# Low parts of a layer's first weights on VectorE, the last tile of a stage normalised there in halves, and a residual scale folded into a power

## The chip, the cores and the metric

The kernel runs on one core of one Trainium2 chip. The metric is the device time of one execution in microseconds (us). Engines are named as the profile names them: PE (TensorE matmul), PEld (its weight load), DVE (VectorE), ACT (ScalarE), POOL (GpSimd), SP (SyncE, whose queue issues nearly all DMAs).

## The reference

Two layers over 512 latent tokens (x) and 256 context tokens (ctx) of width 1024. A layer has a mixing part (one input projection `w_in`, three head groups, one output projection `w_out`) and a channel part (SwiGLU, `w_up` and `w_down`), each with adaLN modulation in front and DeepNorm post-normalisation behind. Cut to what the change touches:

```python
def layer_norm(x, g=None, b=None):
    mu = mean(x); var = mean((x - mu) ** 2)
    y = (x - mu) * rsqrt(var + 1e-6)
    return y if g is None else y * g + b

for l in range(2):
    hl = layer_norm(xl) * (1 + mod_l[:, 1]) + mod_l[:, 0]
    yl = mixing(hl @ w_in[l]) @ w_out[l]
    xl = layer_norm(ALPHA * xl + mod_l[:, 2] * yl, ln1_g[l], ln1_b[l])
    hl = layer_norm(xl) * (1 + mod_l[:, 4]) + mod_l[:, 3]
    xl = layer_norm(ALPHA * xl + mod_l[:, 5] * swiglu(hl), ln2_g[l], ln2_b[l])
    # the context goes the same way in layer 0; layer 1 only reads its normalised, modulated form
```

The output is the latent stream.

## The kernel before, in words

**Tiles and products.** Tokens lie in six tiles of 128 x 1024: tiles 0 and 1 are context, 2 to 5 latent. Every fp32 product is made of three matmuls over a high and a low part of each operand (`mm`; all PE rows stand at L137). A weight arrives by DMA as a "unit" (512 KB, 128 x 1024), in the order that `plan` lists and that `pump` issues on SP's queue when the heap has room. `split` then makes the high part, on ACT (L211) or on POOL (L213), and the low part as source minus high part (`tt`, L206), on DVE or POOL. For a token tile the high part is made at L671 (ACT) and the low part at L206 too. Which engine makes a unit's parts is set by `self.weng` and `self.wsub`. `mixing` sets POOL for the low parts at its start.

**What sets the order.** `STEPS[l]` is a string that orders the steps of the mixing part of layer l, one letter a step. Z, H, D and the like are both steps and switches: D puts later low parts on DVE, O puts them on POOL, H and h put high parts on POOL or ACT. A small letter such as a, e, f runs a piece of the input projection or the gating; Z starts the products of the first units. A scheduler then sets each engine's own order from the data and from buffer reuse, and an engine runs its list strictly in that order.

**Stage ends.** `ends` closes a sub-layer. Per tile it makes the second product (`project`, two halves of 512 columns), adds the residual (L1251 multiplies by the gate, L206 adds), collects statistics (L715), and calls `post_ln`: `ln_end` aggregates (L635), makes the inverse deviation with a multiply-add on DVE (L236) and a power on POOL (L237), multiplies it by ALPHA for the next residual (L639), and two DVE instructions of 128 x 1024 apply it (L683, L684). `normal` then takes statistics of the result (L629, L635, L236, L237), forms the bias (L649, DVE, 128 x 1) and normalises the whole tile on ACT (L650). `modulate` transposes the tile on PE in eight 128 x 128 blocks (rows `aux<-cst,f`), applies scale and shift on ACT (L665), and makes high and low parts. Modulation of a tile is put two tiles later, and the last two tiles' low parts are on DVE, the others' on POOL.

While the last two tiles are being normalised, PE is fed with `fill`: the first products of the next sub-layer on tiles that are ready (128 x 256 rows), in three pieces set by `cuts`. Three ends have a sub-layer behind them: the end of mixing in layer 0 ("mixing-0 end", 255 to 335 us of the span, six tiles), of the channel part in layer 0 ("MLP-0 end", 846 to 935 us, six tiles), of mixing in layer 1 ("mixing-1 end", 1060 to 1127 us, four tiles). The fourth end writes the output and has neither ALPHA nor `normal`.

The first products of layer 1 in the MLP-0 end use the units z0 and z1 (`in1.z0`, `in1.z1`), a2, a3 and, a little later, v0 and v1. At the entry of the mixing-1 end the eight units of `w_out` are scaled by a column of `par` while they are split (L1384 on ACT, L1385 on DVE).

**Head.** `first_mod` modulates the input of layer 0 in eight column blocks k. Per block, context (128 x 256) and latent (128 x 512) go through a DVE multiply-add (L418), an ACT high part (L422) and a low part: latent on DVE, context on POOL (both L206).

## Time and profile before

| what | value |
|---|---|
| device time, median of 3 runs | 1481.41 us (1479.87 to 1483.12) |
| the profiled execution's own time | 1483.5 us |
| its span (first to last instruction) | 1481.4 us |
| PE busy | 1403.3 us, 95% of the span, 7307 matmuls |
| DVE busy | 865.3 us, 58% |
| ACT busy | 517.4 us, 35% |
| POOL busy | 288.2 us, 19% |
| mean granted TensorE clock | 0.975 of full speed |
| DMA | 160.39 MB, 34.5% of 16 engines' span |

An engine row of a timeline gives the start in the span, the time to the end of the last of the merged instructions, the line, the operation with output and inputs, the count, and in brackets the idle time in front with what ended it. `f` and `r` are heap buffers (fp32, and fp32 in the form that PE takes), `smalls` holds 128 x 1 values, `mm` and `aux` are PSUM. The granted clock is 1.00 at 2.4 GHz and 0.50 at 1.2 GHz.

### The profile page before, as it was taken

The page shows a single profiled execution, that of the slowest core. Times are in us where ns is not written, and L with a number is a line of the kernel's source. Part 1 is how long each engine was busy: PE and PEld are TensorE (multiplying, and loading weights), DVE is VectorE, ACT ScalarE, POOL GpSimd, SP SyncE. Part 2 cuts the span into 40 slices and gives each one's busy share as a digit, 9 for nine tenths or more (in the row PEclk, how much of TensorE's full clock was granted, in tenths as well). Part 3 has the DMA queues.
Part 4 walks back from the last instruction along what each step waited for, and adds up shares of the span by engine and source line. Part 5 has one row for each costly group of instructions (what it writes and reads, how often), then busy time and mean ns, then how long its engine had stood idle before and what let it go on. Part 6 is the DMA issues. An engine that isn't in the chain of part 4 may idle for free.

```text
span 1481.4 us, 18151 instructions
## 1 busy us (share of the span) xinstructions
PE 1403.3 (95%) x7307; PEld 1172.6 (79%) x7307; DVE 865.3 (58%) x1230; ACT 517.4 (35%) x719; POOL 288.2 (19%) x199
## 2 busy tenths in 40 slices
PE   6998898999999999999999998997889999999997
PEld 3777876789888888888888877776678888888885
DVE  6638847779248357536226496579786353362427
ACT  4467435345113203112103155785345232232210
POOL 3302323330030030120030055033330112020201
PEclk9999999999999999999999999998899999999999
DMA  9602455044126053371145015013346143342101
GB/s 325 206 15 89 141 187 183 0 147 154 43 66 204 29 153 117 100 222 63 29 128 185 29 53 147 15 43 100 114 143 198 43 128 114 93 121 78 50 15 57
DMA packets 168419, 160.39 MB, mean 108 GB/s; under 512 B 10344, under 2 KB 126536, under 8 KB 168336
## 3 DMA queue, kind: packets, MB, share of 16 engines
q1 hardware_dynamic: 168224, 158.95, 34.5%
q8 instruction: 57, 0.93, 0.3%
q0 software_dynamic: 112, 0.30, 0.1%
q14 instruction: 26, 0.21, 0.0%
HBM read 157.12 MB, written 2.10 MB: 107 GB/s over the span
## 4 chain that ended last, share of the span: by engine, by line
PE 76%; DVE 12%; ACT 5%; issue 4%; POOL 3%; DMA 1%; SPq 0%; DVEq 0%; ACTq 0%; POOLq 0%
PE mm L137 71%; PE aux L137 5%; POOL smalls L237 2%; DVE f L206 1%; DVE f L684 1%; POOL r L206 1%; DVE r L206 1%; DVE f L1251 1%; DVE f L831 1%; DVE smalls L715 1%; ACT f L665 1%; DVE f L828 1%; DVE r L1385 1%; DVE f L830 1%; ACT f L818 1%
## 5 line engine op out<-in xcount | busy, mean ns | idle before, releaser
L137 PE MATMUL mm<-r,r 128*128 128x512 f32 (+1 forms) x6000 | 1198.0, 361 | 20.2 <-DVE f L1251 6.5
L137 PEld LDWEIGHTS mm<-r,r 128*128 128x128 f32 x6000 | 1009.6, 191 | 198.0 <-DVE f L1251 11.3
L211 ACT ACTIVATE r<-f 128x1024 fp32r<-128x1024 f32 (+2 forms) x210 | 195.0, 953 | 560.2 <-PE mm L137 197.2
L206 DVE TENSOR_TENSOR r<-f,r 128x1024 fp32r<-128x1024 f32 (+2 forms) x232 | 252.1, 1109 | 148.4 <-ACT r L211 123.7
L206 POOL TENSOR_TENSOR f<-f,f 128x1024 f32<-128x1024 f32 x40 | 99.6, 2490 | 636.4 <-DVE f L1251 606.2
L1251 DVE TENSOR_TENSOR f<-mm,f 128x512 f32<-128x512 f32 (+1 forms) x80 | 76.3, 953 | 133.2 <-PE mm L137 132.6
L1266 DVE TENSOR_TENSOR f<-mm,f 128x768 f32<-128x768 f32 (+1 forms) x44 | 36.2, 824 | 169.2 <-PE mm L137 167.5
L206 POOL TENSOR_TENSOR r<-f,r 128x512 fp32r<-128x512 f32 (+2 forms) x52 | 90.0, 1738 | 136.9 <-DVE f L828 45.9
L237 POOL TENSOR_TENSOR smalls<-smalls,neghalf 128x1 f32<-128x1 f32 (+3 forms) x61 | 61.9, 1016 | 246.0 <-DVE smalls L236 245.6
L579 DVE SCALAR_TENSOR_TENSOR f<-f,stc,f 128x512 f32<-128x512 f32 x140 | 102.3, 762 | 5.7 <-DMA f<-in_w_mod_dram 4.5
L206 DVE TENSOR_TENSOR f<-f,f 128x512 f32<-128x512 f32 (+1 forms) x70 | 58.3, 835 | 20.2 <-ACT f L799 18.7
L137 PE MATMUL aux<-r,r 128*128 128x256 f32 x480 | 60.7, 288 | 3.6 <-ACT f L1010 3.6
L137 PEld LDWEIGHTS aux<-r,r 128*128 128x128 f32 x480 | 59.7, 196 | 4.9 <-ACT f L1010 3.8
L665 ACT ACTIVATE f<-aux,modT 128x128 f32<-128x128 f32 x128 | 48.4, 464 | 33.6 <-PE aux L137 31.3
L1265 ACT ACTIVATE f<-mm 128x768 f32<-128x768 f32 (+1 forms) x44 | 30.7, 697 | 77.3 <-PE mm L137 77.2
L137 PE MATMUL aux<-cst,f 128*128 128x128 f32 (+1 forms) x239 | 35.3, 284 | 22.7 <-ACT f L650 12.0
L137 PE MATMUL mm<-f,f 128*128 128x512 f32 (+3 forms) x168 | 52.8, 467 | 4.0 <-ACT f L799 3.0
L650 ACT ACTIVATE f<-f,smalls 128x1024 f32<-128x1024 f32 x19 | 23.6, 1244 | 93.2 <-DVE smalls L649 93.2
L137 PEld LDWEIGHTS aux<-cst,f 128*128 128x128 f32 (+1 forms) x239 | 28.1, 144 | 31.4 <-ACT f L650 14.6
L137 PEld LDWEIGHTS mm<-f,f 128*128 128x128 f32 x168 | 30.9, 193 | 21.0 <-issue 8.6
L783 DVE SCALAR_TENSOR_TENSOR f<-mm,par,f 128x255 f32<-128x255 f32 (+3 forms) x48 | 25.7, 611 | 21.8 <-ACT f L777 21.8
L799 ACT ACTIVATE f<-mm,par 128x768 f32<-128x768 f32 x32 | 28.3, 902 | 15.7 <-PE mm L137 10.7
(128 smaller groups left out, 731.1 us busy)
## 6 DMA issues: line engine op xcount, KB each, us to landing
f<-in_w_mod_dram SPq DMA_DIRECT2D x96, 512.0 KB
f<-in_w_up_dram SPq DMA_DIRECT2D x88, 512.0 KB
f<-in_w_down_dram SPq DMA_DIRECT2D x40, 512.0 KB
f<-in_w_in_dram SPq DMA_DIRECT2D x28, 512.0 KB
f<-in_w_out_dram SPq DMA_DIRECT2D x16, 512.0 KB
f<-in_b_mod_dram SPq DMA_DIRECT2D x6, 512.0 KB
f<-in_x_dram SPq DMA_DIRECT2D x4, 512.0 KB
f<-in_ln_g_dram SPq DMA_DIRECT2D x4, 512.0 KB
```

Source lines behind the costliest of these rows:

```text
L137: i = f(*args, **kw)
L206: return eng.tensor_tensor(out=out, in0=a, in1=b, op=op)
L211: i = self.nc.scalar.activation(h, src, AF.Copy)
L237: self.nc.gpsimd.tensor_tensor(out=out, in0=v, in1=self.neghalf[:, 0:n], op=ALU.pow)
L579: nc.vector.scalar_tensor_tensor(out=b.f, in0=w, scalar=c, in1=b.f, op0=ALU.mult, op1=ALU.add)
L650: nc.scalar.activation(n.f, x, AF.Identity, bias=nm, scale=r)
L665: nc.scalar.activation(y.f[:, q * P : (q + 1) * P], ps[:, q * P : (q + 1) * P], AF.Identity, bias=self.modT[:, slot, k, s : s + 1], scale= ...
L783: nc.vector.scalar_tensor_tensor(out=o, in0=ps[:, i0 : i0 + o1 - o0], scalar=w(k), in1=o, op0=ALU.mult, op1=ALU.add)
L799: insts.append(nc.scalar.activation(g.f, ps[:, 256:1024], AF.Sigmoid, bias=par[:, col : col + 1]))
L1251: self.nc.vector.tensor_tensor(out=tb.f, in0=ps[:, c], in1=m[:, c], op=ALU.mult)
L1265: nc.scalar.activation(g.f, pg[:, 256 + lo : 1024], AF.Silu)
L1266: nc.vector.tensor_tensor(out=g.f, in0=pu[:, 256 + lo : 1024], in1=g.f, op=ALU.mult)
```

## The change

There are four edits:

1. The order string of layer 1 gets a D in front and an O behind the f: the low parts of the units used from there to the O are made on DVE instead of POOL.
2. `first_mod` makes the context's eight low parts on DVE instead of POOL.
3. `ln_end` takes ALPHA into the multiply-add in front of the power, (v q + eps q)^(-1/2) with q = 1 / ALPHA^2, and drops L639, 16 instances.
4. `ends` normalises the last tile of each end that isn't the kernel's last with two DVE instructions of 128 x 512 (`normal_halves`, L655 of the changed file) instead of L649 and L650.

```diff
-STEPS = ("feaeZeeppzssz8shgpmOsgs6p7sVsshvUv6HuvDcLmu8F6gHDc8cFwhuNRmtgDmAQmBmP", "ZaHfeepzszVpssvcecegwsvppUDsFuhugsgDsgs6L7NAtQBP")
+STEPS = ("feaeZeeppzssz8shgpmOsgs6p7sVsshvUv6HuvDcLmu8F6gHDc8cFwhuNRmtgDmAQmBmP", "DZaHfOeepzszVpssvcecegwsvppUDsFuhugsgDsgs6L7NAtQBP")
...
-                self.tt(nc.vector if s == 0 else nc.gpsimd, L, y, H.bitcast(F32), ALU.subtract)
+                self.tt(nc.vector, L, y, H.bitcast(F32), ALU.subtract)
...
-        self.rstd(mv[:, 2:3], mv[:, 1:2], 1.0, eps)
-        r = mv[:, 2:3]
-        if scale is not None and scale != 1.0:
-            nc.vector.tensor_scalar(out=mv[:, 3:4], in0=r, scalar1=scale, scalar2=None, op0=ALU.mult)
-            r = mv[:, 3:4]
-        return mv[:, 0:1], r
+        q = 1.0 / (scale or 1.0) ** 2
+        self.rstd(mv[:, 2:3], mv[:, 1:2], q, eps * q)
+        return mv[:, 0:1], mv[:, 2:3]
...
+    def normal_halves(self, x):
+
+        mu, r = self.ln_stats(x, EPS_X)
+        n = self.buf(D)
+        for c in (slice(0, 512), slice(512, 1024)):
+            self.nc.vector.tensor_scalar(out=n.f[:, c], in0=x[:, c], scalar1=mu, scalar2=r, op0=ALU.subtract, op1=ALU.mult)
+        return n
...
-                ns[ti] = self.normal(self.X[ti])
+                ns[ti] = self.normal_halves(self.X[ti]) if i > len(tiles) - 2 else self.normal(self.X[ti])
```

Behind L639 the changed file's line numbers differ: L649 is L646 there, L650 is L647, L665 and L671 are L670 and L676, L683 and L684 are L688 and L689, L715 is L720, L1251 is L1256, L1384 and L1385 are L1389 and L1390.

**First place: DVE in the MLP-0 end, tile 5.** `f_1024_75` is tile 5; `r_1024` outputs of L206 are low parts of weight units, `r_4096_79` the low part of the tokens. DVE before:

```order
L683 SCALAR_TENSOR_TENSOR f_1024_5869<-f_1024_75,smalls,f_1024_457 128x1024
L639 TENSOR_SCALAR smalls<-smalls 128x1
L206 TENSOR_TENSOR r_1024_5257<-f_1024_5513,r_1024_4714 128x1024
L684 SCALAR_TENSOR_TENSOR f_1024_75<-f_1024_5869,smalls,f_1024_5864 128x1024
L629 BN_STATS smalls<-f_1024_75 128x6 x2
L206 TENSOR_TENSOR r_4096_79<-f_512_6294,r_4096_77 128x512
L635 BN_AGGR smalls<-smalls 128x2
L236 TENSOR_SCALAR smalls<-smalls 128x1
L649 SCALAR_TENSOR_TENSOR smalls<-smalls 128x1
L206 TENSOR_TENSOR r_4096_79<-f_512_5991,r_4096_77 128x512
```

and with the change:

```order
L688 SCALAR_TENSOR_TENSOR f_1024_5863<-f_1024_75,smalls,f_1024_457 128x1024
L206 TENSOR_TENSOR r_1024_5251<-f_1024_5507,r_1024_4708 128x1024
L689 SCALAR_TENSOR_TENSOR f_1024_75<-f_1024_5863,smalls,f_1024_5858 128x1024
L206 TENSOR_TENSOR r_1024_6111<-f_1024_131,r_1024_3692 128x1024
L629 BN_STATS smalls<-f_1024_75 128x6 x2
L206 TENSOR_TENSOR r_4096_79<-f_512_6288,r_4096_77 128x512
L635 BN_AGGR smalls<-smalls 128x2
L206 TENSOR_TENSOR r_1024_4421<-f_1024_4625,r_1024_6969 128x1024
L236 TENSOR_SCALAR smalls<-smalls 128x1
L206 TENSOR_TENSOR r_4096_79<-f_512_5985,r_4096_77 128x512
L655 TENSOR_SCALAR f_1024_5863<-f_1024_75,smalls 128x512 x2
L206 TENSOR_TENSOR r_1024_6242<-f_1024_5791,r_1024_6964 128x1024
```

L639 and L649 are gone, two L655 stand in place of ACT's L650, and two low parts of weight units (`L206 r_1024`, 128 x 1024) that POOL made now stand between the second post-norm instruction and the normalisation. On POOL, in the same place, before:

```order
L237 TENSOR_TENSOR smalls<-smalls,neghalf 128x1
L213 TENSOR_SCALAR r_1024_7057<-f_1024_6817 128x1024
L206 TENSOR_TENSOR r_1024_7058<-f_1024_6817,r_1024_7057 128x1024
L206 TENSOR_TENSOR r_4096_79<-f_512_6294,r_4096_77 128x512
L206 TENSOR_TENSOR r_4096_79<-f_512_6275,r_4096_77 128x512
L237 TENSOR_TENSOR smalls<-smalls,neghalf 128x1 x2
L206 TENSOR_TENSOR r_1024_6117<-f_1024_131,r_1024_3698 128x1024
L237 TENSOR_TENSOR smalls<-smalls,neghalf 128x1
L206 TENSOR_TENSOR r_1024_4427<-f_1024_4631,r_1024_6981 128x1024
L206 TENSOR_TENSOR r_1024_6248<-f_1024_5797,r_1024_6976 128x1024
L213 TENSOR_SCALAR r_1024_5517<-f_1024_459 128x1024
```

and with the change:

```order
L237 TENSOR_TENSOR smalls<-smalls,neghalf 128x1
L213 TENSOR_SCALAR r_1024_7045<-f_1024_6805 128x1024
L237 TENSOR_TENSOR smalls<-smalls,neghalf 128x1
L257 MEMSET f_1024_4415 128x1024
L206 TENSOR_TENSOR r_1024_7046<-f_1024_6805,r_1024_7045 128x1024
L206 TENSOR_TENSOR r_4096_79<-f_512_6288,r_4096_77 128x512
L206 TENSOR_TENSOR r_4096_79<-f_512_6269,r_4096_77 128x512
L237 TENSOR_TENSOR smalls<-smalls,neghalf 128x1 x3
L213 TENSOR_SCALAR r_1024_5511<-f_1024_459 128x1024
```

The three low parts of weight units behind the powers (`r_1024_6117`, `r_1024_4427`, `r_1024_6248`) are gone from POOL, the high part of v1 (L213) has moved in front of a power, and v1's low part and tile 3's two stay ahead of the powers of tiles 4 and 5. PE's list changes there only in its pieces: between tile 4's transposes and tile 5's stand 49 products of 128 x 256 (44 before), and behind tile 5's 131 (141 before).

**Second place: DVE at the entry of the mixing-1 end.** L1385 (L1390) makes the low part of a `w_out` unit, `L206 r_1024` that of a `w_up` unit, `f_1024_192` is the last `w_out` unit to arrive. Before:

```order
L1385 SCALAR_TENSOR_TENSOR r_1024_6256<-f_1024_6179,par,r_1024_7826 128x1024
L206 TENSOR_TENSOR r_1024_7844<-f_1024_7816,r_1024_7843 128x1024
L206 TENSOR_TENSOR r_1024_6248<-f_1024_5797,r_1024_7854 128x1024
L1385 SCALAR_TENSOR_TENSOR r_1024_4418<-f_1024_192,par,r_1024_3121 128x1024
L206 TENSOR_TENSOR r_1024_7177<-f_1024_4356,r_1024_4702 128x1024
L1385 SCALAR_TENSOR_TENSOR r_1024_7841<-f_1024_7814,par,r_1024_7839 128x1024
L1251 TENSOR_TENSOR f_512_7884<-mm,f_1024_3453 128x512
```

and with the change:

```order
L1390 SCALAR_TENSOR_TENSOR r_1024_7335<-f_1024_7542,par,r_1024_7798 128x1024
L1390 SCALAR_TENSOR_TENSOR r_1024_6250<-f_1024_6173,par,r_1024_7814 128x1024
L1390 SCALAR_TENSOR_TENSOR r_1024_7820<-f_1024_7621,par,r_1024_7818 128x1024
L1390 SCALAR_TENSOR_TENSOR r_1024_4412<-f_1024_192,par,r_1024_7828 128x1024
L206 TENSOR_TENSOR r_1024_4422<-f_1024_2650,r_1024_7831 128x1024
L206 TENSOR_TENSOR r_1024_2845<-f_1024_7805,r_1024_3887 128x1024
L206 TENSOR_TENSOR r_1024_3978<-f_1024_4294,r_1024_7841 128x1024
L206 TENSOR_TENSOR r_1024_7046<-f_1024_6805,r_1024_4696 128x1024
L1256 TENSOR_TENSOR f_512_7871<-mm,f_1024_3447 128x512
```

The `w_out` parts now stand together, four low parts of `w_up` behind them, and all of it in front of the first residual. On SP's queue one of the two last `w_out` loads is issued earlier, in front of most `w_up` loads.

**Third place: DVE in the mixing-1 end, tile 5.** Before:

```order
L1251 TENSOR_TENSOR f_512_7055<-mm,f_1024_3453 128x512
L206 TENSOR_TENSOR f_1024_75<-f_1024_75,f_512_7055 128x512
L206 TENSOR_TENSOR r_1024_8393<-f_1024_7829,r_1024_7841 128x1024
L715 BN_STATS smalls<-f_1024_75 128x6
L206 TENSOR_TENSOR r_1024_7057<-f_1024_70,r_1024_8500 128x1024
L635 BN_AGGR smalls<-smalls 128x2
L236 TENSOR_SCALAR smalls<-smalls 128x1
L683 SCALAR_TENSOR_TENSOR f_1024_7989<-f_1024_75,smalls,f_1024_3701 128x1024
L639 TENSOR_SCALAR smalls<-smalls 128x1
L684 SCALAR_TENSOR_TENSOR f_1024_75<-f_1024_7989,smalls,f_1024_7850 128x1024
L629 BN_STATS smalls<-f_1024_75 128x6 x2
L577 TENSOR_SCALAR f_512_5388<-f_1024_192,stc 128x512
```

and with the change:

```order
L1256 TENSOR_TENSOR f_512_8016<-mm,f_1024_3447 128x512
L206 TENSOR_TENSOR f_1024_75<-f_1024_75,f_512_8016 128x512
L720 BN_STATS smalls<-f_1024_75 128x6
L635 BN_AGGR smalls<-smalls 128x2
L236 TENSOR_SCALAR smalls<-smalls 128x1
L688 SCALAR_TENSOR_TENSOR f_1024_7973<-f_1024_75,smalls,f_1024_7836 128x1024
L689 SCALAR_TENSOR_TENSOR f_1024_75<-f_1024_7973,smalls,f_1024_7837 128x1024
L629 BN_STATS smalls<-f_1024_75 128x6 x2
L635 BN_AGGR smalls<-smalls 128x2
L236 TENSOR_SCALAR smalls<-smalls 128x1
L577 TENSOR_SCALAR f_512_8408<-f_1024_4350,stc 128x512
L655 TENSOR_SCALAR f_1024_457<-f_1024_75,smalls 128x512 x2
```

Both low parts of `w_up` units are gone from between the second residual and L635 (one stands ahead of it, the others were made at the entry), and nothing stands between the statistics L629 and the multiply-add L236 but L635. On ACT an L211 of a `w_up` unit now stands ahead of tile 5's L670.

## Rows read from the trace of the kernel before

**Rows 1.** The page, part 4: the chain that ended last, by engine.

```profile
PE 76%; DVE 12%; ACT 5%; issue 4%; POOL 3%; DMA 1%; SPq 0%; DVEq 0%; ACTq 0%; POOLq 0%
```

**Rows 2.** Windows of both stretches: columns busy us (count) by engine, granted clock, DMA.

```profile
908.70:912.10 3.40, 3.40 (x17) 3.40 (x17) 0.69 (x1) 3.40 (x8) 2.05 (x1) 0.50 0.21 37
...
1113.50:1120.30 6.80, 5.02 (x23) 5.01 (x24) 6.80 (x11) 5.71 (x12) 0.00 (x0) 0.50 0.91 275
```

**Rows 3.** Timeline, PE, MLP-0 end: start, us, instruction xcount, [idle before <-releaser].

```profile
897.06 1.09 PE L137 MATMUL aux<-cst,f 128*128 128x128 f32 x8 [2.24 <-ACT f L650]
...
908.56 1.89 PE L137 MATMUL aux<-cst,f 128*128 128x128 f32 x8 [3.65 <-ACT f L650]
```

**Rows 4.** Timeline, DVE, MLP-0 end, tiles 4 and 5.

```profile
895.57 0.16 DVE L649 SCALAR_TENSOR_TENSOR smalls<-smalls 128x1 f32<-128x1 f32 x1 [1.95 <-POOL smalls L237]
...
895.71 1.28 DVE L683 SCALAR_TENSOR_TENSOR f<-f,smalls,f 128x1024 f32<-128x1024 f32 x1
...
898.66 3.40 DVE L684 SCALAR_TENSOR_TENSOR f<-f,smalls,f 128x1024 f32<-128x1024 f32 x1
...
904.94 2.29 DVE L649 SCALAR_TENSOR_TENSOR smalls<-smalls 128x1 f32<-128x1 f32 x1 [0.66 <-POOL smalls L237]
...
920.57 1.53 DVE L783 SCALAR_TENSOR_TENSOR f<-mm,par,f 128x254 f32<-128x254 f32 x3 [5.90 <-ACT f L777]
```

**Rows 5.** Timeline, POOL, MLP-0 end.

```profile
888.85 6.18 POOL L206 TENSOR_TENSOR r<-f,r 128x1024 fp32r<-128x1024 f32 x3
...
898.03 2.94 POOL L206 TENSOR_TENSOR r<-f,r 128x1024 fp32r<-128x1024 f32 x1 [0.63 <-ACT r L211]
904.36 0.55 POOL L237 TENSOR_TENSOR smalls<-smalls,neghalf 128x1 f32<-128x1 f32 x1 [3.38 <-DVE smalls L236]
```

**Rows 6.** Timeline, ACT, MLP-0 end.

```profile
901.13 1.08 ACT L211 ACTIVATE r<-f 128x1024 fp32r<-128x1024 f32 x1
907.26 1.24 ACT L650 ACTIVATE f<-f,smalls 128x1024 f32<-128x1024 f32 x1 [5.05 <-DVE smalls L649]
```

**Rows 7.** Timeline, PE, mixing-0 end.

```profile
333.24 1.09 PE L137 MATMUL aux<-cst,f 128*128 128x128 f32 x8 [1.26 <-ACT f L650]
```

**Rows 8.** Timeline, ACT, mixing-0 end.

```profile
334.60 1.06 ACT L211 ACTIVATE r<-f 128x1024 fp32r<-128x1024 f32 x1 [1.42 <-DMA f<-in_w_up_dram]
```

**Rows 9.** Timeline, PE, entry and last tile of the mixing-1 end.

```profile
1049.00 30.39 PE L137 MATMUL mm<-r,r 128*128 128x512 f32 x123 [1.42 <-ACT r L996]
...
1105.62 3.11 PE L137 MATMUL mm<-r,r 128*128 128x256 f32 x24
1112.16 1.09 PE L137 MATMUL aux<-cst,f 128*128 128x128 f32 x8 [3.42 <-ACT f L650]
1115.28 15.03 PE L137 MATMUL mm<-r,r 128*128 128x256 f32 x89 [2.03 <-ACT r L671]
```

**Rows 10.** Timeline, DVE, entry of the mixing-1 end.

```profile
1060.58 1.28 DVE L1385 SCALAR_TENSOR_TENSOR r<-f,par,r 128x1024 fp32r<-128x1024 f32 x1
1062.89 0.69 DVE L1251 TENSOR_TENSOR f<-mm,f 128x512 f32<-128x512 f32 x1 [1.04 <-PE mm L137]
```

**Rows 11.** Timeline, DVE, last tile of the mixing-1 end.

```profile
1099.28 0.69 DVE L1251 TENSOR_TENSOR f<-mm,f 128x512 f32<-128x512 f32 x1 [2.17 <-PE mm L137]
...
1102.50 1.20 DVE L206 TENSOR_TENSOR r<-f,r 128x1024 fp32r<-128x1024 f32 x1
...
1108.36 0.47 DVE L577 TENSOR_SCALAR f<-f,stc 128x512 f32<-128x512 f32 x1
```

**Rows 12.** Timeline, SP's queue, entry of the mixing-1 end.

```profile
1053.33 0.89 SPq L1346 DMA_DIRECT2D f<-in_w_out_dram  x2
```

**Rows 13.** Timeline, DVE, head of the program.

```profile
36.98 0.40 DVE L418 TENSOR_SCALAR f<-f,modT 128x256 f32<-128x256 f32 x1
37.30 0.68 DVE L206 TENSOR_TENSOR r<-f,r 128x512 fp32r<-128x512 f32 x1
```

**Rows 14.** Timeline, PE, head of the program.

```profile
35.68 1.22 PE L137 MATMUL mm<-r,r 128*128 128x256 f32 x3 [0.41 <-POOL r L206]
```

More of the change, by code (lines that the diff above doesn't have):

```diff
@@ L51 @@
 MIX_RESERVE = (12000, 9000)
-STEPS = ("feaeZeeppzssz8shgpmOsgs6p7sVsshvUv6HuvDcLmu8F6gHDc8cFwhuNRmtgDmAQmBmP", "ZaHfeepzszVpssvcecegwsvppUDsFuhugsgDsgs6L7NAtQBP")
+STEPS = ("feaeZeeppzssz8shgpmOsgs6p7sVsshvUv6HuvDcLmu8F6gHDc8cFwhuNRmtgDmAQmBmP", "DZaHfOeepzszVpssvcecegswvppUDsFuhugsgDsgs6L7NAtQBP")
 PARAMS_AT = 5
```

## The prediction

> **What bounds the kernel now.** I read the chain of waits first: PE is 76% of it, DVE 12%, ACT 5%, POOL 3% [rows 1]. So a gain must come from places where PE stands still or runs slowly, and a DVE microsecond elsewhere costs nothing. I then went through PE's timeline of each stretch that the edits touch, and from each PE gap back to the engine named in brackets. Two gaps are large, and both lie in front of the transposes of a stage's last tile: 3.65 us in the MLP-0 end [rows 3] and 3.42 us in the mixing-1 end [rows 9], each released by ACT's L650. The same gap in the mixing-0 end is 1.26 us [rows 7]. Last I read the windows: soon after each of the two large gaps there is a stretch at a granted clock of 0.50, which is 1.2 of 2.4 GHz, of 3.40 and 6.80 us [rows 2]. The transposes behind the first gap show it: 1.89 us for eight, where the tile before took 1.09 [rows 3].
>
> **MLP-0 end, edits 1, 3 and 4.** From the start of tile 5's L683 at 895.71 [rows 4] to its transposes at 908.56 [rows 3] are 12.85 us, all of it a chain on DVE, POOL and ACT. Step by step with the change:
> - L684 took 3.40 us while POOL made a low part at the same time (898.03, 2.94 us); its twin L683 took 1.28 [rows 4, 5]. That low part leaves POOL: -2.1.
> - L649, one column wide, took 2.29 us beside the next POOL low part (904.88, which ran 2.34), and 0.16 for tile 4 [rows 4]. It is removed, and so is what stretched it: -2.3.
> - L650, 1.24 us on ACT [rows 6], gives way to two L655 on DVE. No row has that form with two column operands; the nearest is L577, one TENSOR_SCALAR of 128x512, at 0.47 us [rows 11], so two are 0.9: -0.3. The bound above is 0.69 each, the time of a 128x512 DVE operation that reads two tensors (the residual in [rows 10]): +0.1.
> - L639 goes: one column wide like L649, 0.16 us [rows 4], and a gap: -0.2.
> - Two low parts of 128x1024 now stand in the chain: 2 x 1.20 [rows 11] = +2.4.
>
> The sum is -2.5. Before L683, tile 4's power waited behind three POOL low parts, 6.18 us from 888.85, and DVE idled 1.95 us for it [rows 4, 5]. Those three stay in front of that power, but POOL's L213 of v1 comes earlier: between 0 and -1.2 (its length and a gap); I take -0.6. Tile 5's transposes thus come 3.1 us earlier, and ten products more are done in front of them (141 behind them before, 131 now): 10 x 0.13 from the 24 that took 3.11 [rows 9] = -1.3, of which I count -1.1 since the last product's tail is in that mean. In all **-4.2**, ends -1.5 (POOL's turn gains nothing and the DVE list waits for ACT once) and -7 (the half clock of 908.7 to 912.1 goes too: 17 products where full clock does twice as many, half of 3.4 us).
>
> A rule of the chip bears on this. The rows above show DVE and POOL stretching each other; POOL's power takes 0.55 us alone [rows 5]. The Trainium skill (SBUF — State Buffer, Who interferes with whom) says that a VectorE instruction with two SBUF inputs and a GpSimd instruction that reads SBUF exclude each other, whichever issued first holding the shared ports for its whole length; L684's 3.40 us agrees. By that rule DVE's low part of tile 4, put right behind L236, would hold back tile 5's power in the new order by about one such operation, and the sum here would be some 0.7 us smaller.
>
> **Mixing-1 end, edits 3 and 4, and what the new order moves.** From the last residual at 1099.28 [rows 11] to the transposes at 1112.16 [rows 9]: 12.88 us. Two low parts leave (2 x 1.20 [rows 11]), L639 (0.2), an L577 and a tile low part in front of the power (0.47 [rows 11] plus 0.6), and L649 with L650 become two L655 (-0.5): -4.2 together. But PE is busy with 24 products until 1108.73 [rows 9], so of the 3.42 us gap at most 3.4 can go. The next gap, 2.03 us behind the transposes for ACT's L671 [rows 9], stays. I take **-3.0**; ends -1 (below, a load that is late) and -5.5 (the half clock goes too: PE was busy 5.02 us of those 6.8 [rows 2], and half of that is 2.5).
>
> **Entry of the mixing-1 end.** PE's 123 products take 30.39 us [rows 9], waiting now and then for a part of `w_out`; the last one is done at 1060.58 + 1.28, and the first residual follows 1.0 us later, released by PE [rows 10]. The last two loads are issued together at 1053.33 [rows 12]; with the change one of them comes earlier, so one L1385 and a low part (1.28 and 1.20) leave the time behind the last landing: -2.5 at best. Four low parts of `w_up` now stand in front of the first residual, 4 x 1.20, of which 1.04 us of idle time [rows 10] and the free third PSUM buffer hide most: up to +1. I take **-1.0**.
>
> **Mixing-0 end.** Six L639 on DVE's list: 0.2 each, of which I count a third, since PE waits for DVE only at some residuals: -0.4. The last tile gains the 0.5 of the two L655, but ACT has an L211 in front of that tile's L665 that waits for a load until 334.60 [rows 8]: -0.4. **-0.8**, ends 0 and -2.
>
> **Head, edit 2.** PE waited 0.41 us for a POOL low part [rows 14]. On DVE each 128x256 low part costs about 0.40 (the multiply-add of that size [rows 13]; above, 0.68, the 128x512 one). Four of them per half of the head are 1.6 us more on a DVE that has no idle time there, and what POOL stretched comes back. I take **-0.3**, ends +1 and -1. The second half is covered by PE's other products, and v0's low part, 1.2 us that edit 1 puts on DVE, by the 5.90 us that DVE idles in front of the convolutions [rows 4]; if POOL's high part of v0 came last there, it would cost 1.2.
>
> **Sum.** -4.2 - 3.0 - 1.0 - 0.8 - 0.3 = -9.3 us. The profiled execution took 1483.5, which becomes 1474.2; it stood 2.1 above the median 1481.4, so the median becomes **1472**. The heap also hands out other buffers, and loads in the last channel part move by some microseconds; nothing in the profile gives that a sign, and I leave 1.5 either way. What a measurement here can tell from no change is about 0.2%, 3 us.
>
> **Rivals.**
> - *The gain goes further* (1467.5): the half-clock stretches behind the two gaps go with them, -1.7 and -2. For it: each followed a gap of over 3 us. Against: by my times gaps of 1 to 2 us stay, and no row here says how short a gap leaves the clock up. 0.2.
> - *Half of it comes* (1476.5): tile 5's chains shorten, but DVE's new low parts hold back the powers and ACT's turn comes late; MLP-0 end -2.5, mixing-1 end -1.5, the rest -1. 0.2.
> - *A new wait takes the old one's place* (1479.5, no change that can be told): in the mixing-1 end ACT's list now has an L211 of a `w_up` unit in front of tile 5's L665. If that load lands after 1108.7 every microsecond later is lost; at 1112 the stage gains nothing. For it: the mixing-0 end shows just this, 1.42 us at 334.60 [rows 8], and DMA is at 0.91 in 1113 to 1120 [rows 2]. With nothing at the entry and +1 in the head: -2. 0.12.
> - *Slower* (1485): in the MLP-0 end two weight low parts stand ahead of L655 on a DVE that runs in order, so tile 5 waits for their ACT splits, and these for their `w_in` loads. By my times the second split must begin by about 900.5. ACT split the later one at 901.13 without having to wait for it [rows 6], so it had landed by then. From 904.5 on the stage gains nothing, and it would have to be 912 for the whole to be 3 us slower. 0.05.
>
> **How the numbers follow.** The forecast, between 1469 and 1475, has 0.43. Forecast, the larger gain and the half gain all lie over 3 us below 1481.4: faster 0.83. The new wait gives 0.12 for the same, the last 0.05 for slower. The range reaches from the larger gain, 1467, to 1478.5, where half the gain ends; it leaves out the two last cases and a little below.
>
> **What would show it.** Right: in the MLP-0 end the gap in front of tile 5's transposes falls from 3.65 to under 3 us while 49 products stand ahead, DVE's L689 takes 1.3 us, L655 0.45 to 0.7 each; in the mixing-1 end the 3.42 us gap is below 0.5; both stretches, timed from their first transposes, are shorter by 3 to 5 us each. Wrong: a DVE L206 in front of L655 that waits for ACT, an ACT L211 in front of tile 5's L670 that waits for a load, the same half-clock stretches behind shorter gaps, or PE waiting for DVE in the head.

## The result, and the profile with the change

The changed kernel takes **1467.2 us**, the median of 4 runs (1465.46 to 1467.72), beside 1481.12 for the kernel before on the same chip: ratio 0.9899, 95% interval 0.9887 to 0.9911. The forecast was 1472, in a range of 1467.0 to 1478.5. So faster was right, the gain is 14 us where 9.3 were forecast, and the time stands just above the range's low end, on the figure of the rival *the gain goes further*, though, as will be seen, only in part for its reason.

One correction stands ahead of everything. The order string in the diff above has one slip: behind `cece` the changed file has `gsw`, where the diff shows `gws`. **The change has a fifth edit:** the step w, layer 1's gating maps, is put one step later, behind a scan step s. The lists of instructions and all runs are of the true file; the prediction's sum has no term for this edit. It will be called edit 5.

The profiled execution took 1467.0 us, its span is 1465.2, the mean clock 0.978. The page, its totals and chain:

```profile
PE 1397.2 (95%) x7307; PEld 1169.5 (80%) x7307; DVE 870.1 (59%) x1229; ACT 514.4 (35%) x716; POOL 271.4 (19%) x187
...
PE 75%; DVE 11%; ACT 5%; issue 3%; POOL 3%; DMA 2%; SPq 0%; DVEq 0%; ACTq 0%; POOLq 0%
```

PE is busy 6 us less than before with the same 7307 matmuls, POOL 17 us less, DVE 5 more. Since every trace of this study holds the same 7307 matmuls, the start of the matmul of one number can be set against its start before; how this difference grows over a stretch is what the stretch gained. The table in the next section has it for all kernels. For the change: MLP-0 end -6.8, the second scan's gates -4.5, in front of the output projection -2.5, mixing-0 end -0.8, mixing-1 end -0.7, its entry +1.8, head and time modulation -2.3 (of which chance is most, below).

**MLP-0 end.** Timeline with the change, tiles 4 and 5:

```profile
891.96 1.28 DVE L688 SCALAR_TENSOR_TENSOR f<-f,smalls,f 128x1024 f32<-128x1024 f32 x1
...
893.55 1.09 PE L137 MATMUL aux<-cst,f 128*128 128x128 f32 x8 [1.90 <-ACT f L647]
894.29 1.28 DVE L689 SCALAR_TENSOR_TENSOR f<-f,smalls,f 128x1024 f32<-128x1024 f32 x1
...
894.39 6.11 PE L137 MATMUL mm<-r,r 128*128 128x256 f32 x49
...
899.84 0.93 POOL L237 TENSOR_TENSOR smalls<-smalls,neghalf 128x1 f32<-128x1 f32 x1 [6.20 <-DVE smalls L236]
900.80 1.00 DVE L655 TENSOR_SCALAR f<-f,smalls 128x512 f32<-128x512 f32 x2 [0.45 <-POOL smalls L237]
...
901.50 1.08 PE L137 MATMUL aux<-cst,f 128*128 128x128 f32 x8 [0.99 <-DVE f L655]
```

This answers to [rows 3 to 6]. L689 takes 1.28 us where L684 took 3.40. Two L655 take 1.00, and PE starts on the first half 0.70 us after they began. From L688 to tile 5's transposes it is now 901.50 - 891.96 = 9.54 us, before 12.85. PE's gap there is 0.99 us, behind 49 products, as many as the order showed. The windows of both old half-clock stretches [rows 2], with the change:

```profile
901.50:905.00 3.50, 3.50 (x30) 3.46 (x31) 1.86 (x3) 2.84 (x8) 0.00 (x0) 1.00 0.39 107
905.00:912.00 7.00, 7.00 (x60) 7.00 (x59) 2.26 (x4) 2.21 (x4) 1.05 (x1) 1.00 0.27 91
1097.50:1104.30 6.80, 4.65 (x20) 4.36 (x21) 6.76 (x11) 5.78 (x9) 0.00 (x0) 0.50 0.43 132
```

Behind the MLP-0 end the clock is now 1.00; behind the mixing-1 end a stretch of 6.80 us at 0.50 is still there. [rows 2] leave out one more half-clock stretch of before, behind tile 4's transposes (0.50 from 898.5 to 901.9 us). The change doesn't have it either. `wo5` and `all4_u1dve` (below), with the same four edits here, do have one there (0.50 from 892.7 to 896.1 us) and still gain 6.1 and 6.5 us at this end, so it counts for little.

**Mixing-1 end.** Timeline with the change, last tile:

```profile
1090.97 3.11 PE L137 MATMUL mm<-r,r 128*128 128x256 f32 x24
...
1093.10 1.00 DVE L655 TENSOR_SCALAR f<-f,smalls 128x512 f32<-128x512 f32 x2 [0.44 <-POOL smalls L237]
...
1093.92 1.04 PE L137 MATMUL aux<-cst,f 128*128 128x128 f32 x8
...
1094.18 1.06 ACT L211 ACTIVATE r<-f 128x1024 fp32r<-128x1024 f32 x1
...
1095.14 0.61 ACT L676 ACTIVATE r<-f 128x512 fp32r<-128x512 f32 x1
...
1097.38 0.64 ACT L676 ACTIVATE r<-f 128x512 fp32r<-128x512 f32 x1
...
1098.07 1.01 PE L137 MATMUL mm<-r,r 128*128 128x256 f32 x3 [3.12 <-ACT r L676]
...
1098.92 1.09 ACT L211 ACTIVATE r<-f 128x1024 fp32r<-128x1024 f32 x1
1099.87 0.66 ACT L676 ACTIVATE r<-f 128x512 fp32r<-128x512 f32 x1
1099.91 0.68 DVE L206 TENSOR_TENSOR r<-f,r 128x512 fp32r<-128x512 f32 x1
...
1100.65 2.72 PE L137 MATMUL mm<-r,r 128*128 128x256 f32 x11 [1.58 <-DVE r L206]
```

Tile 5's transposes start without a gap (3.42 us before, [rows 9]). But behind them PE stands still twice, 3.12 and 1.58 us, where before it was once 2.03. The 24 products are used up, and what is next needs tile 5's own halves: ACT runs L670, two L211, L676 in turn, DVE the low part. The gap moved behind the transposes. Further ahead a gap has grown that no term spoke of, in front of the 72 products between the transposes of tiles 3 and 4; before, and with the change:

```profile
1093.53 11.47 PE L137 MATMUL mm<-r,r 128*128 128x512 f32 x72 [0.74 <-DVE f L1251]
```

```profile
1078.70 11.64 PE L137 MATMUL mm<-r,r 128*128 128x512 f32 x72 [1.60 <-DVE f L1256]
```

**Two places that no term spoke of.** At 970 us before, the second scan's gates. Timeline before:

```profile
970.35 1.89 POOL L213 TENSOR_SCALAR r<-f 128x1024 fp32r<-128x1024 f32 x1 [38.58 <-ACT f L799]
...
971.36 4.70 DVE L206 TENSOR_TENSOR f<-f,f 128x768 f32<-128x768 f32 x2
...
972.32 2.92 POOL L206 TENSOR_TENSOR r<-f,r 128x1024 fp32r<-128x1024 f32 x1
...
976.15 2.48 ACT L799 ACTIVATE f<-mm,par 128x768 f32<-128x768 f32 x3 [4.99 <-DVE f L206]
...
977.11 2.93 PE L137 MATMUL mm<-f,f 128*128 128x256 f32 x4 [2.71 <-ACT f L799]
```

and its window:

```profile
977.00:980.40 3.40, 3.29 (x6) 1.99 (x7) 0.96 (x1) 1.97 (x4) 0.27 (x1) 0.50 0.00 0
```

DVE's two products of 128x768 took 4.70 us while POOL made unit u1's low part (2.92). ACT waited 4.99 us for them, PE 2.71, and its four products behind the gap, at a granted clock of 0.50, took 2.93 (sixteen take 5.42 with the change, at 1.00). So two things were lost here: the gap, and about half of a 3.4 us stretch. The same place with the change:

```profile
960.52 5.42 PE L137 MATMUL mm<-f,f 128*128 128x256 f32 x16
...
961.52 1.81 DVE L206 TENSOR_TENSOR f<-f,f 128x768 f32<-128x768 f32 x2
961.70 2.54 POOL L213 TENSOR_SCALAR r<-f 128x1024 fp32r<-128x1024 f32 x1 [39.74 <-ACT f L942]
...
964.33 2.37 POOL L206 TENSOR_TENSOR r<-f,r 128x1024 fp32r<-128x1024 f32 x1
```

DVE's two take 1.81 us and PE runs 16 products without a gap. Now POOL is the one held up: L213 takes 2.54 us where it took 1.89. POOL's low part (964.33, 2.37) now stretches DVE's next pair, 4.07 us from 965.16 on, but PE has other products then and does not wait. At 1036 us before, in front of the output projection:

```profile
1030.77 1.28 DVE L1385 SCALAR_TENSOR_TENSOR r<-f,par,r 128x1024 fp32r<-128x1024 f32 x1
...
1032.57 2.58 DVE L1385 SCALAR_TENSOR_TENSOR r<-f,par,r 128x1024 fp32r<-128x1024 f32 x2
...
1035.08 0.68 DVE L206 TENSOR_TENSOR f<-f,f 128x512 f32<-128x512 f32 x1
...
1035.91 1.84 PE L137 MATMUL aux<-ones,f 128*128 128x1 f32 x8 [10.96 <-DVE f L206]
```

and with the change:

```profile
1019.09 1.84 PE L137 MATMUL aux<-ones,f 128*128 128x1 f32 x8 [8.46 <-DVE f L206]
```

Before, three L1385 (1.28 and 2.58 us) stood on DVE's list ahead of the L206 that PE waited for. In the new order one L1390 stands at 1023.41 and four of 4.86 us together at 1037.45, behind that L206, and the wait is 8.46 us, not 10.96.

### The profile page after: what moved, and what is told of

Read it like the earlier page. It is cut to its first block, busy times and chain, and to the rows that moved or that the text cites. A ratio compares the mean times of both kernels' runs of the same rounds, so it can differ in the third digit from the quotient of the medians.

```text
span 1465.2 us, 18157 instructions
## 1 busy us (share of the span) xinstructions
PE 1397.2 (95%) x7307; PEld 1169.5 (80%) x7307; DVE 870.1 (59%) x1229; ACT 514.4 (35%) x716; POOL 271.4 (19%) x187
## 4 chain that ended last, share of the span: by engine, by line
PE 75%; DVE 11%; ACT 5%; issue 3%; POOL 3%; DMA 2%; SPq 0%; DVEq 0%; ACTq 0%; POOLq 0%
PE mm L137 71%; PE aux L137 4%; POOL smalls L237 2%; DVE f L206 1%; POOL r L206 1%; DVE f L689 1%; DVE r L206 1%; DVE f L833 1%; DVE f L836 1%; DVE f L1256 1%; DMA f<-in_w_mod_dram 1%; DVE smalls L720 1%; ACT f L670 1%; ACT f L826 1%; ACT f L823 1%
## 5 line engine op out<-in xcount | busy, mean ns | idle before, releaser
L137 PEld LDWEIGHTS mm<-r,r 128*128 128x128 f32 x6000 | 1008.0, 191 | 199.8 <-DVE f L1256 12.3
L211 ACT ACTIVATE r<-f 128x1024 fp32r<-128x1024 f32 (+2 forms) x210 | 195.8, 952 | 569.0 <-PE mm L137 232.3
L206 DVE TENSOR_TENSOR r<-f,r 128x1024 fp32r<-128x1024 f32 (+2 forms) x244 | 259.4, 1087 | 149.2 <-ACT r L211 124.9
L206 POOL TENSOR_TENSOR f<-f,f 128x1024 f32<-128x1024 f32 x40 | 99.7, 2492 | 638.4 <-DVE f L1256 608.3
L1256 DVE TENSOR_TENSOR f<-mm,f 128x512 f32<-128x512 f32 (+1 forms) x80 | 76.2, 953 | 130.3 <-PE mm L137 129.1
L206 POOL TENSOR_TENSOR r<-f,r 128x512 fp32r<-128x512 f32 (+2 forms) x40 | 72.2, 1815 | 134.3 <-ACT r L211 56.1
L206 DVE TENSOR_TENSOR f<-f,f 128x512 f32<-128x512 f32 (+1 forms) x70 | 59.6, 855 | 18.8 <-ACT f L804 16.5
L670 ACT ACTIVATE f<-aux,modT 128x128 f32<-128x128 f32 x128 | 48.4, 464 | 36.4 <-PE aux L137 31.0
L647 ACT ACTIVATE f<-f,smalls 128x1024 f32<-128x1024 f32 x16 | 19.9, 1241 | 83.8 <-DVE smalls L646 83.8
```

Source lines behind the costliest of these rows:

```text
L137: i = f(*args, **kw)
L206: return eng.tensor_tensor(out=out, in0=a, in1=b, op=op)
L211: i = self.nc.scalar.activation(h, src, AF.Copy)
L647: nc.scalar.activation(n.f, x, AF.Identity, bias=nm, scale=r)
L670: nc.scalar.activation(y.f[:, q * P : (q + 1) * P], ps[:, q * P : (q + 1) * P], AF.Identity, bias=self.modT[:, slot, k, s : s + 1], scale= ...
L1256: self.nc.vector.tensor_tensor(out=tb.f, in0=ps[:, c], in1=m[:, c], op=ALU.mult)
```

## The experiments

Twelve kernels ran, in three groups, each beside the kernel before on the same chip (its medians 1482.74, 1482.42 and 1483.11). First each part of the change was taken out of it, then edits 1, 3, 4 and 5 were each put alone into the kernel before. The gain by stretch, in us, from one profiled execution each against the trace of before (columns: stretch, in times of before's span; the kernels by their names below; "before" is the kernel before once more):

| stretch | change | before | wo1 | wo2 | wo3 | wo4 | wo5 | only1 | only3 | only4 | only5 | u1dve | all4_ u1dve |
|---|---|---|---|---|---|---|---|---|---|---|---|---|---|
| 0 to 35.7, start | -1.2 | -1.3 | -1.1 | 0.0 | 1.5 | -0.1 | -1.4 | -0.4 | -0.5 | 0.1 | 0.0 | 0.3 | 0.8 |
| to 43.9, head, first half | -0.7 | -0.5 | -0.7 | -0.2 | -1.1 | -0.3 | -0.6 | 0.0 | -0.2 | 0.2 | -0.6 | 0.0 | -1.1 |
| to 73.6, head, second half | -0.5 | 0.0 | -0.5 | 0.0 | -0.5 | -0.5 | -0.5 | 0.0 | 0.0 | 0.0 | 0.0 | 0.0 | -0.5 |
| to 261 | 0.1 | -1.9 | 0.1 | -1.7 | -4.1 | -0.8 | 0.2 | -0.1 | -1.6 | 0.2 | -2.0 | -0.1 | -2.9 |
| to 350, mixing-0 end | -0.8 | 0.0 | -2.0 | -1.9 | -0.1 | -1.1 | -1.9 | 0.0 | -0.9 | -0.7 | 0.0 | 0.0 | -1.2 |
| to 914, MLP-0 end | -6.8 | 0.6 | -5.0 | -6.5 | -5.5 | -6.4 | -6.1 | -5.7 | -4.2 | 1.1 | 0.6 | 0.1 | -6.5 |
| to 1024, second scan's gates | -4.5 | 0.1 | -4.5 | -4.5 | -4.5 | -4.5 | 0.0 | -1.6 | -0.1 | -0.1 | -4.5 | -3.7 | -3.7 |
| to 1042, before output projection | -2.5 | 0.0 | -2.5 | -2.5 | -2.5 | -2.5 | 0.0 | 0.0 | 0.0 | 0.0 | -2.5 | 0.0 | -0.4 |
| to 1078, entry | 1.8 | 0.3 | 1.6 | 1.2 | 2.5 | 2.2 | 0.9 | 0.1 | -0.1 | -0.2 | 2.0 | 0.1 | 0.8 |
| to 1126, mixing-1 end | -0.7 | 0.2 | -0.7 | -0.8 | 2.0 | -0.4 | -2.2 | 0.2 | -0.3 | -0.4 | 1.8 | 0.1 | -1.6 |
| sum | -15.7 | -2.6 | -15.3 | -16.9 | -12.3 | -14.3 | -11.7 | -7.5 | -8.1 | 0.1 | -5.3 | -3.4 | -16.3 |

**Chance in the table.** The column "before" is the same program as what it is compared with. Over 1 us it shows only in the first 36 us (-1.3) and in 73.6 to 261 (-1.9): there half-clock stretches lie at other places in each execution. At 205.0 to 212.5 us the clock was 0.54 before, 0.89 in the second execution of before, 0.67 in the change and 1.00 in `wo3`. So these two rows say nothing about the edits. In the other rows, too, each value is from one execution: half of a half-clock stretch of 3.4 us is 1.7 us, and a load that lands 1 us later can move the mixing-0 end by as much (both are seen below).

> The kernel before once more, for a second trace: in its first trace a half-clock stretch at 21.2 to 24.6 us of the span cost 1.6 us ahead of anything that the change touches. Chance: another execution doesn't have it there, or has it elsewhere. Otherwise it is there again. The half-clock stretches behind the two large gaps (898.5, 908.7, 1113.5 us) and at 977 us are expected again in either case.

Measured: one run, 1480.86 us. It gives the column just used.

**Taking one part out of the change.** `wo1` (edit 1 undone):

```diff
-"DZaHfOeepzszVpssvcecegswvpp
+"ZaHfeepzszVpssvcecegswvpp
```

> The change without the D and the O of the order string: the low parts of layer 1's first units go back to POOL, all else stays. The changed kernel took 1467.2 us. Theory A (each stage's gain belongs to the edit that touches it): the MLP-0 end, 6.7 us shorter in PE's sequence with all edits, loses 3 to 5 of them, since DVE's L689 and POOL's low parts collide again; the 4.5 us that were gained behind it, at the gates of the second scan (PE waited 2.7 us for ACT L799 there before and half the clock followed), also hang on what POOL has to do and come back: 1473 to 1477. Theory B (those 4.5 us and the 1.6 us at the program's head are chance of the clock or of buffer places): only the MLP-0 end loses, 1470 to 1472.

Measured: 1468.13 us, 0.9906 (0.9891 to 0.9921), no slower than the change that can be told. The MLP-0 end still gains 5.0. Tile 5's chain is 9.66 us, as with the change.

`wo4` (edit 4 undone):

```diff
-ns[ti] = self.normal_halves(self.X[ti]) if i > len(tiles) - 2 else self.normal(self.X[ti])
+ns[ti] = self.normal(self.X[ti])
```

> The change with the last tiles normalised on ACT again (no halves). Theory A: tile 5's transposes come 0.5 us later in each of three ends, and ACT's turn is longer; together 1 to 2.5 us, 1468 to 1470. Theory B: the same in the ends, but the places of all later buffers move too, so the 4.5 us behind the MLP-0 end may go with it: up to 1474.

Measured: 1466.75 us, 0.9887 (0.9867 to 0.9908), the same as the change. PE in the MLP-0 end:

```profile
894.76 8.45 PE L137 MATMUL mm<-r,r 128*128 128x256 f32 x56
903.05 1.04 PE L137 MATMUL aux<-cst,f 128*128 128x128 f32 x8
```

56 products stand in front of tile 5's transposes, and PE does not wait for them at all, although ACT normalises the tile. The halves buy nothing here.

`wo2` (edit 2 undone):

```diff
-self.tt(nc.vector, L, y, H.bitcast(F32), ALU.subtract)
+self.tt(nc.vector if s == 0 else nc.gpsimd, L, y, H.bitcast(F32), ALU.subtract)
```

> The change with the context's low parts in the head on POOL again. Theory A: the head's two batches in PE's sequence were 1.0 and 0.45 us shorter with the edit, so 1.4 us go: 1468.6. Theory B: the head's whole 3.0 us belong to it: 1470.

Measured: 1467.19 us, 0.9901 (0.9885 to 0.9916), the same as the change. In the table the second half of the head gains 0.5 in exactly the six kernels that have edit 2 there; a gain of that size is below what the runs can tell.

`wo3` (L639 back, edit 3 undone):

```diff
-q = 1.0 / (scale or 1.0) ** 2
-self.rstd(mv[:, 2:3], mv[:, 1:2], q, eps * q)
-return mv[:, 0:1], mv[:, 2:3]
+self.rstd(mv[:, 2:3], mv[:, 1:2], 1.0, eps)
+r = mv[:, 2:3]
+if scale is not None and scale != 1.0:
+    nc.vector.tensor_scalar(out=mv[:, 3:4], in0=r, scalar1=scale, scalar2=None, op0=ALU.mult)
+    r = mv[:, 3:4]
+return mv[:, 0:1], r
```

> The change with ALPHA multiplied on DVE again (L639 back). Theory A: sixteen instructions with their place in a chain, 0.2 us each where the chain is waited for: 0.7 us in the mixing-0 end, 0.5 in each of the others, 1468.5 to 1469.5. Rival: since without edit 1 and without edit 4 the MLP-0 end kept 5.0 and 6.4 of its 6.7 us, L639's removal might be what it hangs on, then the MLP-0 end is back by 3 us or more, 1471.

Measured: 1470.32 us, 0.992 (0.9905 to 0.9934): some 3 us are lost, though the interval just overlaps the change's. By the table 0.7 of it is in the mixing-0 end, 1.3 in the MLP-0 end, 2.6 in the mixing-1 end. Most of the last is the clock: behind a longer gap in front of the 72 products it read 0.50 from 1081.2 to 1084.6 us, where the change has no such stretch, and the products take 13.12 us, not 11.64:

```profile
1080.05 13.12 PE L137 MATMUL mm<-r,r 128*128 128x512 f32 x72 [2.04 <-DVE f L1259]
```

`wo5` (edit 5 undone):

```diff
-cecegswvpp
+cecegwsvpp
```

> The change with one letter pair of layer 1's order string put back: the changed string also has the step w (gating maps) behind a scan step s, gsw for gws, and here it is gws again. Theory A: three low parts of the output projection stand again on DVE in front of the last residual sum of squares before the output projection, PE waits 2.5 us longer there (10.96 us before, 8.46 with the change), and the 1.8 us that the entry of the mixing-1 end lost come back: 1467 to 1469, and the 4.5 us at the second scan stay. Theory B: the swap is what moved the second scan, and its 4.5 us go too: 1471 to 1473.

Measured: 1470.8 us, 0.992 (0.9906 to 0.9935), some 3 us lost as well, again with an interval that just overlaps. Timeline at the second scan's gates:

```profile
960.01 1.89 POOL L213 TENSOR_SCALAR r<-f 128x1024 fp32r<-128x1024 f32 x1 [38.56 <-ACT f L804]
...
961.03 4.70 DVE L206 TENSOR_TENSOR f<-f,f 128x768 f32<-128x768 f32 x2
...
961.98 2.92 POOL L206 TENSOR_TENSOR r<-f,r 128x1024 fp32r<-128x1024 f32 x1
...
966.77 1.94 PE L137 MATMUL mm<-f,f 128*128 128x256 f32 x4 [2.71 <-ACT f L804]
```

The pair on DVE is back at 4.70 us and PE's gap at 2.71; the gain at the output projection is gone too (0.0). What it gets back is the entry, +0.9 instead of +1.8, and the mixing-1 end, -2.2 instead of -0.7; the gap in front of the 72 products is 0.55 us there.

**One part alone in the kernel before.** `only5` (edit 5 alone, the reverse of the diff above, on the kernel before):

> The kernel before with the swapped pair gsw alone. Theory C and A: 3.4 us at the second scan, 2.5 us in front of the output projection, about 2 us given back at the entry of the mixing-1 end and behind: 1477 to 1479. If the swap needs the other edits, 1482.

Measured: 1477.84 us, 0.9968 (0.9956 to 0.998). Gates -4.5, output projection -2.5, entry +2.0, mixing-1 end +1.8: some half of what edit 5 gains is given back behind it. In the mixing-1 end it is as in `wo3`: a gap of 2.01 us in front of the 72 products, then the clock at 0.50 from 1088.4 to 1091.8 us.

`u1dve` (the kernel before, with only u1's low part moved from POOL to DVE, which the letters D and O around w do):

```diff
-cecegwsvpp
+cecegDwOsvpp
```

> The kernel before, with the low part of one weight unit (u1, step w of layer 1) on DVE instead of POOL; it stands on DVE behind the two residual products of 128x768 in front of the scan's second gates, and nothing else moves on any engine. Theory C (with the swap, POOL's parts of u1 start 0.2 us behind those two DVE products instead of 1.0 us ahead of them, because u1's high part gets another buffer; before, POOL's low part of 2.9 us held the shared port and the two took 4.70 us instead of 1.81): here the low part isn't on POOL, the two take 1.8 to 2.8 us, PE's gap of 2.71 us and the half clock behind it mostly go, 1.2 us of low part come in behind: 3 to 4.4 us less in PE's sequence at that point, 1478 to 1479. Theory D (the swap works by the order of the scan's steps, not by POOL): the two still take 4.7 us and the time is that of before, 1482.

Measured: 1479.55 us, 0.9979 (0.9969 to 0.9988). One instruction of 128x1024 is moved, no step is. Timeline:

```profile
971.50 2.54 DVE L206 TENSOR_TENSOR f<-f,f 128x768 f32<-128x768 f32 x2
...
973.97 1.21 DVE L206 TENSOR_TENSOR r<-f,r 128x1024 fp32r<-128x1024 f32 x1
...
975.10 1.56 PE L137 MATMUL mm<-f,f 128*128 128x256 f32 x4 [0.56 <-ACT f L799]
```

The pair takes 2.54 us and PE's gap is 0.56: -3.7 at the gates and 0 everywhere else. It was mostly POOL's low part that stretched the pair (2.2 of the 2.9 us; the 0.7 left goes with POOL's high part, which stayed), not the place of w as such.

`only1` (edit 1 alone), `only3` (edit 3 alone), `only4` (edit 4 alone), each on the kernel before:

> The kernel before with the D and the O alone (first low parts of layer 1 on DVE, no swap). The MLP-0 end was 6.8 us shorter with the whole change, 5.0 without this edit, 6.4 without the halves, 5.5 without the folded ALPHA. Theory E (any one of them shortens tile 5's chain by over a microsecond, and then the two half-clock stretches of that end, 3.4 us together, go at once, so the edits are substitutes): 4 to 6 us in that end and nothing elsewhere, 1476 to 1478. Rival F (the edits add up and none is enough alone): 2 us or less, 1480.

> The kernel before with ALPHA folded into the power alone. Theory E: 3 to 5 us in the MLP-0 end, 0.5 to 0.8 in the mixing-0 end, about 0.5 in the mixing-1 end, 1477 to 1478. Rival F: 0.2 us for each tile whose chain is waited for, 1 to 2 us in all, 1480.5 to 1481.5.

> The kernel before with the last tiles normalised in halves on DVE alone. Theory E: 3 to 5 us in the MLP-0 end, and in the mixing-1 end PE's 3.42 us gap shrinks by 0.5 to 1: 1476.5 to 1478. Rival F: 0.5 to 1 us in each of the three ends, 1479.5 to 1481.

Measured: `only1` 1475.88 us, 0.9958 (0.9944 to 0.9973); `only3` 1475.43, 0.9954 (0.9938 to 0.9971); `only4` 1482.39, 0.9997 (0.9985 to 1.0009). In the MLP-0 end -5.7, -4.2 and +1.1; together, in the change, -6.8. Edits 1 and 3 thus do much the same thing there. The +1.1 of `only4` goes with a longer half-clock stretch behind tile 4's transposes, 0.50 from 895.7 to 902.5 us. The -1.6 of `only1` at the gates is the clock as well. The pair still takes 4.69 us and PE's gap is 2.71 as before, but the clock reads 1.00 behind it, and the four products take 1.56 us instead of 2.93:

```profile
970.97 1.56 PE L137 MATMUL mm<-f,f 128*128 128x256 f32 x4 [2.71 <-ACT f L799]
```

Timeline of `only3`:

```profile
893.73 6.33 POOL L206 TENSOR_TENSOR r<-f,r 128x1024 fp32r<-128x1024 f32 x2
...
894.40 3.39 DVE L681 SCALAR_TENSOR_TENSOR f<-f,smalls,f 128x1024 f32<-128x1024 f32 x1
...
900.01 1.00 POOL L237 TENSOR_TENSOR smalls<-smalls,neghalf 128x1 f32<-128x1 f32 x1
901.04 0.16 DVE L646 SCALAR_TENSOR_TENSOR smalls<-smalls 128x1 f32<-128x1 f32 x1 [0.44 <-POOL smalls L237]
...
902.53 1.10 PE L137 MATMUL aux<-cst,f 128*128 128x128 f32 x8 [1.68 <-ACT f L647]
```

POOL's two low parts now run together ahead of tile 5's power (6.33 us). One still stretches the second post-norm instruction to 3.39, but it no longer stands beside the normalisation, and L646, at 901.04, takes 0.16 us right behind the power. In `only1` they are gone from POOL altogether. In `only4` they stay where they were (L658 is L655 there):

```profile
904.60 4.84 POOL L206 TENSOR_TENSOR r<-f,r 128x1024 fp32r<-128x1024 f32 x2
904.67 5.05 DVE L658 TENSOR_SCALAR f<-f,smalls 128x512 f32<-128x512 f32 x2 [0.67 <-POOL smalls L237]
...
907.38 0.63 PE L137 MATMUL aux<-cst,f 128*128 128x128 f32 x4 [2.02 <-DVE f L658]
...
909.87 1.09 PE L137 MATMUL aux<-cst,f 128*128 128x128 f32 x4 [1.85 <-DVE f L658]
```

Two POOL low parts start just ahead of the two halves, and these take 5.05 us instead of 1.00; PE waits twice, 2.02 and 1.85. What was the stretched L649 and then ACT is now two stretched halves.

`all4_u1dve` (the change, with `cecegDwOsvpp` in place of edit 5's `cecegswvpp`):

> All edits of the change, but in place of the swapped pair the one low part of u1 on DVE. From the parts measured so far (PE's sequence 11.7 us shorter without the swap, and 3.1 to 3.7 more for u1's low part on DVE when it stands alone): 1467 to 1468, the time of the change, reached without the swap's 2.5 us in front of the output projection and without what it gives back at the entry of the mixing-1 end and at tile 5 there. If theory C of the second scan were wrong, 1470.5.

Measured: 1466.58 us, 0.9892 (0.9875 to 0.9909). It cannot be told from the change. Gates -3.7, output projection -0.4, mixing-1 end -1.6. No kernel of the study is measurably better than the change. The mixing-1 end goes from +2.0 (`wo3`) to -2.2 us (`wo5`), and much of that hangs on edit 5. The gap in front of the 72 products is 1.59 to 2.04 us in the six kernels that have it and 0.55 to 0.74 in the others. The two of the six where it is 2.0 (`wo3`, `only5`) have the extra half-clock stretch. What stays open is which DVE instruction makes PE wait there longer.

**Why edit 5 moves POOL's start.** The order of POOL's instructions with buffer places (the number behind `r_` or `f_` is the column in the heap), before and with the change:

```
L206 TENSOR_TENSOR r_19200_1024_1681<-f_19200_1024_1039,r_1024_1024_7339 128x1024
L206 TENSOR_TENSOR r_19200_1024_1681<-f_19200_1024_1039,r_7168_1024_7335 128x1024
```

u1's high part gets column 1024 before and 7168 with the change. A scan gate of ACT's L799 stands in column 1024 before it, and POOL's L213 is released by ACT L799; at 7168 it is released by ACT L942. It then starts 0.18 us behind DVE's pair, where before it started 1.01 us ahead of it. `only5` and `wo1` to `wo4` have 7168 and the short pair, `wo5` has 1024 and the long one. What a kernel with column 7168 and w in its old place would do was not tried.

## Why the prediction was right or wrong

- **Mixing-0 end**, -0.8 forecast: -0.8. PE's gap fell from 1.26 [rows 7] to 0.35 us. Each half of the term shows alone (`only3` -0.9, `only4` -0.7). That the figure agrees is luck: `wo1`, `wo2` and `wo5`, with the same two edits here, gain 1.9 to 2.0. In the change ACT's L211, ahead of the last tile's L670, waited 5.64 us for its load, until 332.25 us (330.93 to 331.49 in those three), and PE waited 0.34 and 0.24 us more behind it.
- **MLP-0 end**, -4.2 forecast: -6.8. The mechanism was right, two sizes were not. The chain from L683 to the transposes became 3.3 us shorter, not 2.5: the two low parts cost it 2.0 instead of 2.4, PE starts behind the first half of L655 (-0.3 more), and dropping L639 lets DVE start earlier (-0.4 more). The power is the other way, 0.93 us beside a DVE low part of 0.68, not 0.55. That is the Trainium skill's rule on the shared ports (SBUF — State Buffer, Who interferes with whom), weighed ahead at 0.7 us, and the trace agrees in kind with 0.4. The list ahead of L688 gave 0.6 as forecast (3.75 us of start, less the 3.1 by which everything in front was earlier). The larger miss is the half clock, 1.7 us, which I left to a rival: the clock read 1.00 behind tile 5 gaps of 0 to 1.7 us (`wo4`, the change, `only1`, `wo1`, `only3`) and 0.50 behind those of 3.65 and 3.84 (the two executions of before) and behind the waits of 2.02 and 1.85 in `only4`. With -0.8 and -1.7 the -4.2 become -6.7. The sum also put 2.3 us to L649's removal. With edit 1 or edit 3 alone the same instruction (L646 in `only3`) takes 0.16 us, so edit 4 adds nothing; the sum priced the steps one by one, as if they added up.
- **Mixing-1 end**, -3.0 forecast: -0.7. The step that failed is "the next gap stays". The gap in front of tile 5's transposes went as forecast, to none, but the 24 products in front had been the cover for both gaps. With the transposes earlier nothing is left to run while ACT and DVE make tile 5's parts, 3.12 and 1.58 us. And even without edit 5 the first gap does not close: in `wo5` and `all4_u1dve` it is 2.40 and 2.43 us, the next 1.61 and 2.01. With edit 5 the gap in front of the 72 products takes 0.9 us more. An ACT L211 in front of L676 was named as a sign of the new wait; it shows, but ACT did not wait for its load there.
- **Entry**, -1.0 forecast: +1.8. With edit 5 the high part of a `w_out` unit (ACT L1389, 1.14 us at 1031.66) stands right ahead of the L1001 that PE waits for, and the wait is 2.24 us (1.42 before, [rows 9]; 2.24 in `only5`, 1.43 and 1.42 in `wo5` and `all4_u1dve`). The clock then reads 0.50 for the first 6.0 us of PE's run, before for 3.1. Edit 5 alone brings +2.0 here (`only5`). `all4_u1dve` and `wo5`, without it, still show +0.8 and +0.9, so the sign was wrong in any case.
- **Head**, -0.3 forecast: the second half -0.5, the first within chance, since the kernel before moved by 0.5 there from one execution to the next.
- **Not in the sum:** -4.5 at the gates and -2.5 at the output projection, both edit 5. This is the step that failed most: the sum holds nothing for the stretch between 955 and 1040 us, because the changed string was read for D and O only and the view of DVE and POOL there was not read. The four edits by themselves are `wo5`, at 1470.8 us, near the 1472 of the forecast. But that too is luck: its stretches read -1.9, -6.1, +0.9 and -2.2 where the sum has -0.8, -4.2, -1.0 and -3.0.
- **Rivals.** *The gain goes further* has the right time by accident: one of its two half-clock stretches went, the other is there, and the rest is mostly edit 5. *A new wait* took a place in the mixing-1 end, though in another form. *Slower* did not show: no L206 ahead of L655 waits for ACT.

The terms by measurement: -0.8 - 6.8 - 0.7 + 1.8 - 4.5 - 2.5 = -13.5. With the -2.3 of the first 261 us, most of it chance, that is the profiled execution's -15.7 by the table (up to a rounding); by the medians it is -13.9.

## What to carry to other kernels

Look for DVE instructions that take two or three times their usual time, and read what POOL does in those microseconds: moving one 128x1024 POOL low part off such a place (`u1dve`) shortened its stretch by 3.7 us, and moving those of the first units (`only1`) the MLP-0 end by 5.7, while splitting or moving the victim (edit 4 alone) was worth nothing. When a gap in front of a last tile is closed, count the work that remains to cover the next gap behind it. And compare an order string letter by letter: two exchanged letters moved four places in the program.
